# Twelve more hand-overs between the column steps of the block inverses and their transposes

## The chip, the core and the metric

The kernel runs on one core of a Trainium2 chip. Five engines work side by side, each through its own instructions in order: TensorE (PE in the profile, with its weight loads as PEld), VectorE (DVE), ScalarE (ACT), GpSimd (POOL) and SyncE (SP), which starts nearly all transfers. The metric is the device time of one execution in microseconds; lower is better.

## What is computed

One layer of a diffusion backbone on 1024 latent tokens and 256 context tokens, width 1024. An adaptive RMSNorm is followed by one projection of all 1280 tokens, whose columns feed two groups of heads: a gated DeltaNet (a convolution over five tokens, normalised q and k, and a scan over chunks of 64 tokens in the reference, forward and backward) and a neighbourhood attention on a grid 64 wide. An output projection and a SwiGLU feed-forward net follow. The piece around the change is the triangular system of each chunk:

```python
px = modulate(rms_norm(x, norm1_w[i]), sh1, sc1) @ w_in[i]
pc = modulate(rms_norm(ctx, norm1_w[i]), csh1, csc1) @ w_in[i]
...
m = jnp.where(strict, jnp.einsum("bhncd,bhnmd->bhncm", kb, k) * decay, 0.0)
a_mat = jnp.eye(CHUNK, dtype=f32) + m
u = lax.linalg.triangular_solve(a_mat, v * beta[..., None], left_side=True, lower=True, unit_diagonal=True)
w = lax.linalg.triangular_solve(a_mat, kb * jnp.exp(gam)[..., None], left_side=True, lower=True, unit_diagonal=True)
```

The kernel takes chunks of 128 tokens, so there are ten, two of context and eight of latents. It inverts the 32x32 blocks on the diagonal of each chunk's matrix first and builds the rest of the inverse from products of them.

## The kernel before, in words

**Projection.** The columns are worked through as a list of jobs (`jobs`). A Block is 128 columns of one kind: `k`, `q`, `v` and `z` belong to the DeltaNet, `nk` and `nq` to the attention. A Wide is a piece of the attention's values. Around the change they stand in this order: nk0, nk1, nk2, Wide, nk3, nq0, nq1, nq2, q0, q1, q2, q3. Each value is split in a high and a low part, and each product is made of three matmuls: high by high, low by high, high by low (`hh,whi`, `hl,whi`, `hh,wlo` in the rows). For nq and q a Block is eight steps over the 1024 rows (`KT`), with two column halves of 512 tokens, so 48 matmuls of 128x512 by the helper at L98 into two PSUM banks called `blk`, of which there are four.

**Around a Block.** At its start the weights of the job behind it are fetched: SP starts the load into `wraw` (L215; one buffer), ACT casts it to `whi` (L216; two buffers), and the low part `wlo` is made from it. At its end ACT empties the banks into `cacc` (L462). The normalisation of nk and nq squares `cacc` on ACT (L503), sums it in matmuls of `cr` with a constant `cst` into the PSUM banks called `m`, with one in a bank called `pr` for nk, takes Ln (L520) and Exp (L522, L524) of that on ACT, with table loads between them, multiplies on DVE (L527), casts on ACT (L532, L539), and SP stores it (L545). There are two banks `m`.

**Background work.** After each of the eight steps of a Block the loop calls `bg.step`, once up to q0 and three times from q1 on (`turn`); at each tile of a Wide it is called with 2, or 5. `bg` is a queue of generators; one step runs the first of them to its next `yield`, and what it issues up to there stands in program order at that place. The framework's scheduler then sets each engine's order from the program order and the dependences, without a time of its own for what a wait will cost.

The first generator is `block_inverses`. It transposes the 32x32 blocks into a layout in which 80 matrices times four blocks lie beside each other (`N`, on 80 partitions), and eliminates column by column on DVE: 30 steps of a multiply (L913) and an add (L915), with a `yield` after each. Then DVE sets the diagonal to one (L918), and there is one `yield`. Then come 32 transposes on PE (L102) out of that layout, four to a bank `m`, each bank emptied by an ACT copy into `WK` (L926), with a `yield` after each eight transposes. At last, for each of the two scan directions, DVE transposes (L932) and scales (L935), and SP stores both results in `x_d` in DRAM (L934, L937), with a `yield` after each direction.

The second generator is `preps`. It fetches decays `e` (L962), the products of keys `kk` (L963) and the block inverses `xc` (L964) of one chunk and direction; ACT copies `xc` into `fx` (L976) and takes the exponential of `e` (L980); DVE multiplies `kk` by it (L981); and PE makes the products `pr` (L98) that fill the inverse below its diagonal blocks, with an ACT copy (L991) and DVE copies between them. Only the four preps of the context chunks may begin before the blocks nq0 to q2 are done; the others wait for the last q block.

**Other transfers.** While nk3 and nq0 run, SP also issues the copies that gather the attention windows of the values (L1058, `vw_d` from `nv_d`).

Of the kernel before, what the change touches and what calls it, by code (L numbers as in the profile page):

```python
# [87 lines left out]
def hybrid(ctx, tc, a, dbg):  # L88
# [304 lines left out]
    with ExitStack() as bs:  # L393
# [459 lines left out]
        def block_inverses():  # L853
            with ExitStack() as gs:
# [61 lines left out]
                    yield  # L916
                flat = N.rearrange("p b r c -> p b (r c)")
                dve.memset(flat[:P, :, 0:1024:33], 1.0)  # L918
                yield
                U = WK.rearrange("p d u i -> p (d u) i")  # L920
                for i0 in range(0, 32, 4):
                    p = bank()
# [151 lines left out]
        for n in range(2, len(jobs) + 2):  # L1074
            j = jobs[n] if n < len(jobs) else None
            if n == inv:
                bg2.drain()
                bg2s.close()
                early.close()
                psum.append(bs.enter_context(tc.tile_pool(name="psa", bufs=1, space=PSUM)))  # L1080
                bg.add(block_inverses())
                bg.add(preps())
# [700 lines left out]
```

## Time and profile before

| what | value |
|---|---|
| three runs | 1526.71, 1526.71, 1532.21 us |
| median of the runs | 1526.71 us |
| the profiled execution, whole | 1526.16 us |
| its span in the trace | 1524.4 us |
| instructions in it | 23483 |
| PE busy, share of the span | 96% |
| DVE busy | 66% |
| ACT busy | 47% |
| POOL busy | 12% |
| mean granted clock of TensorE | 0.992 |

All times are microseconds from the span's start. A timeline row gives the start, the duration, the engine, the line, the operation, the output and the inputs by the program's names, the shape, how many equal instructions are grouped, and in brackets the engine's idle time ahead of it with what ended it. Matmuls overlap in the pipeline, so the pace of a series is read from the starts of its rows, not from the durations. A row of a window gives for each engine the busy share (the number of instructions that start in it), then the clock that the throttle granted to TensorE as a share of full speed, the share in which the DMA engines were busy, and GB/s. "blk L98" means output `blk`, line 98.

### The profile page before, as it was taken

The page shows a single profiled execution, that of the slowest core. Times are in us where ns is not written, and L with a number is a line of the kernel's source. Part 1 is how long each engine was busy: PE and PEld are TensorE (multiplying, and loading weights), DVE is VectorE, ACT ScalarE, POOL GpSimd, SP SyncE. Part 2 cuts the span into 40 slices and gives each one's busy share as a digit, 9 for nine tenths or more (in the row PEclk, how much of TensorE's full clock was granted, in tenths as well). Part 3 has the DMA queues.
Part 4 walks back from the last instruction along what each step waited for, and adds up shares of the span by engine and source line. Part 5 has one row for each costly group of instructions (what it writes and reads, how often), then busy time and mean ns, then how long its engine had stood idle before and what let it go on. Part 6 is the DMA issues. An engine that isn't in the chain of part 4 may idle for free.

```text
span 1524.4 us, 23483 instructions
## 1 busy us (share of the span) xinstructions
PE 1460.5 (96%) x8365; PEld 1206.5 (79%) x8365; DVE 1004.4 (66%) x1898; ACT 710.6 (47%) x1387; POOL 184.8 (12%) x253
## 2 busy tenths in 40 slices
PE   5999998999999999998899989999999999999998
PEld 3789787778877778887787878888888888888887
DVE  4787579354677427779986388765655556599642
ACT  5443362683366546566642374333333334354441
POOL 0154610342134300000100000000000000000000
PEclk9999999899999999999999999999999999999999
DMA  9377223654477789998539315333233335798742
GB/s 367 112 229 238 61 78 122 234 152 168 132 217 253 223 280 278 285 273 237 164 102 330 109 35 186 111 104 104 104 104 103 104 104 173 246 364 294 235 152 83
DMA packets 209830, 276.29 MB, mean 181 GB/s; under 512 B 15968, under 2 KB 116912, under 8 KB 208688
## 3 DMA queue, kind: packets, MB, share of 16 engines
q1 hardware_dynamic: 208992, 274.41, 55.7%
q8 instruction: 66, 1.08, 0.3%
q14 instruction: 52, 0.43, 0.1%
q10 hardware_dynamic: 720, 0.37, 0.1%
HBM read 209.93 MB, written 68.98 MB: 183 GB/s over the span
## 4 chain that ended last, share of the span: by engine, by line
PE 75%; DVE 11%; DMA 4%; issue 4%; ACT 4%; POOL 1%; SPq 0%; POOLq 0%; DVEq 0%; ACTq 0%
PE ps L98 50%; PE blk L98 12%; PE sc L98 4%; PE pr L98 3%; PE m L98 3%; PE sc L102 2%; DVE tt L913 2%; DVE N L915 2%; DVE cacc L471 1%; PE m L102 1%; PE pm L98 1%; ACT bt L340 1%; DVE bt L337 1%; DMA wad<-wa 1%; DMA wraw<-w_out 1%
## 5 line engine op out<-in xcount | busy, mean ns | idle before, releaser
L98 PE MATMUL ps<-hT,uhi 128*128 128x512 f32 x496 | 147.1, 391 | 3.1 <-ACT hT L1534 3.1
L98 PE MATMUL ps<-lT,uhi 128*128 128x512 f32 x496 | 146.3, 389 | 0.0
L98 PE MATMUL ps<-hT,ulo 128*128 128x512 f32 x496 | 146.2, 389 | 0.0
L98 PE MATMUL blk<-hh,whi 128*128 128x512 f32 (+1 forms) x456 | 139.5, 398 | 2.2 <-ACT hh L714 1.5
L98 PE MATMUL ps<-hB,uhi 128*128 128x512 f32 x436 | 129.7, 391 | 0.0
L98 PE MATMUL ps<-lB,uhi 128*128 128x512 f32 x436 | 129.3, 390 | 0.0
L98 PE MATMUL blk<-hh,wlo 128*128 128x512 f32 (+1 forms) x456 | 129.1, 377 | 0.0
L98 PE MATMUL ps<-hB,ulo 128*128 128x512 f32 x436 | 128.9, 389 | 0.0
L98 PE MATMUL blk<-hl,whi 128*128 128x512 f32 (+1 forms) x456 | 128.7, 376 | 0.0
L1410 ACT CAST uhi<-ws 128x512 fp32r<-128x512 f32 x91 | 54.8, 623 | 153.0 <-PE ps L98 87.6
L1410 ACT CAST uhi<-wq 128x512 fp32r<-128x512 f32 x101 | 60.6, 621 | 135.3 <-PE ps L98 73.4
L98 PEld LDWEIGHTS ps<-hT,uhi 128*128 128x128 f32 x496 | 93.1, 188 | 22.7 <-ACT hT L1534 3.5
L1411 DVE TENSOR_TENSOR ulo<-wq,uhi 128x512 fp32r<-128x512 f32 x101 | 67.4, 688 | 66.0 <-ACT uhi L1410 37.6
L98 PEld LDWEIGHTS ps<-lT,uhi 128*128 128x128 f32 x496 | 93.3, 188 | 19.5
L98 PEld LDWEIGHTS ps<-hT,ulo 128*128 128x128 f32 x496 | 93.1, 188 | 19.3
L98 PEld LDWEIGHTS ps<-hB,uhi 128*128 128x128 f32 x436 | 82.1, 188 | 17.6 <-issue 0.5
L98 PEld LDWEIGHTS ps<-lB,uhi 128*128 128x128 f32 x436 | 82.1, 188 | 17.1
L98 PEld LDWEIGHTS ps<-hB,ulo 128*128 128x128 f32 x436 | 81.8, 188 | 17.0
L98 PEld LDWEIGHTS blk<-hh,wlo 128*128 128x128 f32 x456 | 80.5, 190 | 17.7 <-issue 2.5
L98 PEld LDWEIGHTS blk<-hl,whi 128*128 128x128 f32 x456 | 81.0, 190 | 15.7
L98 PEld LDWEIGHTS blk<-hh,whi 128*128 128x128 f32 x456 | 77.6, 193 | 18.9 <-ACT hh L714 3.1
L337 DVE CUSTOM_DVE_ANT_0 bt<-sc,bt 128x640 f32<-128x640 f32 x64 | 52.5, 822 | 49.1 <-issue 39.4
(332 smaller groups left out, 3057.9 us busy)
## 6 DMA issues: line engine op xcount, KB each, us to landing
wq<-w_fo SPq DMA_DIRECT2D x99, 256.0 KB
wq<-w_gu SPq DMA_DIRECT2D x88, 256.0 KB
wad<-wa SPq DMA_DIRECT2D x64, 256.0 KB
bt<-rpb SPq DMA_DIRECT2D x64, 192.0 KB
t_d<-g SPq DMA_DIRECT2D x22, 512.0 KB
fr<-t_d SPq DMA_DIRECT2D x44, 256.0 KB
f_d<-g SPq DMA_DIRECT2D x33, 256.0 KB
fr<-f_d SPq DMA_DIRECT2D x33, 256.0 KB
```

The lines of the kernel that those rows point to most:

```text
L98: i = nc.tensor.matmul(*args, **kw)
L102: i = nc.tensor.transpose(*args, **kw)
L337: dve.tensor_tensor_reduce(bt, sc[:, u * 640:u * 640 + 640], bt, 1.0, -3.0e38, OP.add, OP.max, m[:, 0:1])
L340: act.activation(bt, bt, AF.Exp, bias=m[:, 1:2], accum_out=m[:, 2:3])
L471: dve.scalar_tensor_tensor(acc[:, d0:d1], p[:, d0 + o - s0:d1 + o - s0], cw[:, blk, tap:tap + 1], acc[:, d0:d1], op0=OP.mult, op1=OP.add)
L913: dve.tensor_tensor(t, N[:P, :, 0:c, c:c + 1].to_broadcast([P, 4, c, w]), N[:P, :, c:c + 1, c + 1:32].to_broadcast([P, 4, c, w]), OP.mult)
L915: dve.tensor_tensor(N[:P, :, 0:c, c + 1:32], N[:P, :, 0:c, c + 1:32], t, OP.add)
L1410: act.copy(hi, self.raw[key])
L1411: dve.tensor_tensor(lo, self.raw[key], hi.bitcast(F32), OP.subtract)
```

## The change

Where the generator of the block inverses gave back control once between the diagonal's memset and the transposes, it does so thirteen times.

```diff
                 flat = N.rearrange("p b r c -> p b (r c)")
                 dve.memset(flat[:P, :, 0:1024:33], 1.0)
-                yield
+                for _ in range(13):
+                    yield
                 U = WK.rearrange("p d u i -> p (d u) i")
                 for i0 in range(0, 32, 4):
                     p = bank()
```

No instruction is added or removed. With one background step per step of a Block, the transposes stand a block and a half later in the program, and all that follows in the queue, the stores of `x_d` and the preps, moves with them. Lines behind the change have a number that is one higher (the ACT copy L926 is L927).

The first place is PE at the transposes, in before. The `blk` rows are matmuls of the projection, `m<-cst,N` the transposes; these rows lie in the second half of block nq0.

```order
L98 MATMUL blk<-hh_139,wlo 128x512 x2
L98 MATMUL blk<-hh_414,whi 128x512
L102 MATMUL m<-cst,N 128x80 x2
L98 MATMUL blk<-hh_414,whi 128x512
L98 MATMUL blk<-hl_415,whi 128x512 x2
L102 MATMUL m<-cst,N 128x80 x6
L98 MATMUL blk<-hh_414,wlo 128x512
L102 MATMUL m<-cst,N 128x80 x8
L98 MATMUL blk<-hh_414,wlo 128x512
L102 MATMUL m<-cst,N 128x80 x8
L98 MATMUL blk<-hh_416,whi 128x512
L102 MATMUL m<-cst,N 128x80 x8
```

The same place in the program after the change, now in the last quarter of block nq1 (`hh_416` to `hh_420`); with the last two rows the next block, nq2, begins (`hh_133`), and `m<-cr,cst` is the sum of the normalisation of nq0. The last eight transposes stand four matmuls further on.

```order
L98 MATMUL blk<-hh_416,wlo 128x512 x2
L102 MATMUL m<-cst,N 128x80 x8
L98 MATMUL blk<-hh_418,whi 128x512 x2
L98 MATMUL blk<-hl_419,whi 128x512 x2
L98 MATMUL blk<-hh_418,wlo 128x512 x2
L102 MATMUL m<-cst,N 128x80 x8
L98 MATMUL blk<-hh_420,whi 128x512 x2
L98 MATMUL blk<-hl_421,whi 128x512 x2
L98 MATMUL blk<-hh_420,wlo 128x512 x2
L102 MATMUL m<-cst,N 128x80 x8
L98 MATMUL blk<-hh_133,whi 128x512 x2
L98 MATMUL m<-cr,cst 128x512 x2
```

From 25 matmuls of nq0 ahead of the first transpose it has become all 48 of nq0 and 36 of nq1, and the groups of eight stand six matmuls apart where they stood one apart.

The second place is ACT at the copies that empty the transposes' banks, in before; `cacc<-blk` empties a block, and the rows of L520 and L524 are the normalisation of nk3.

```order
L503 ACTIVATE cr<-cacc 128x1280
L926 COPY WK<-m 128x80x4 x8
L216 CAST whi<-wraw 128x1024
L462 ACTIVATE cacc<-blk 128x512 x2
L520 ACT_TABLE_LOAD
L520 ACTIVATE cr<-m,bias 128x256
```

The same stretch of ACT after the change.

```order
L503 ACTIVATE cr<-cacc 128x1280
L216 CAST whi<-wraw 128x1024
L462 ACTIVATE cacc<-blk 128x512 x2
L520 ACT_TABLE_LOAD
L520 ACTIVATE cr<-m,bias 128x256
L520 ACTIVATE cr<-m,bias 128x512
L520 ACTIVATE cr<-pr,bias 128x512
L503 ACTIVATE cr<-cacc 128x1024
L524 ACT_TABLE_LOAD
L524 ACTIVATE cr<-cr 128x1280
L532 CAST hl_2414<-cacc 128x1280
L927 COPY WK<-m 128x80x4 x4
```

The copies stood ahead of the cast of the weights of nq2 and now stand behind it and behind the whole normalisation of nk3.

The third place is PE at the first products of the preps. In before they stand at the start of block nq2 (`hh_133`), behind the sums of the normalisation of nq0.

```order
L98 MATMUL blk<-hh_420,wlo 128x512 x2
L98 MATMUL m<-cr,cst 128x512 x2
L98 MATMUL pr<-fx_2475,kk 128x96 x4
L98 MATMUL blk<-hh_133,whi 128x512 x2
L98 MATMUL blk<-hl_134,whi 128x512 x2
L98 MATMUL pr<-y_2471,kk 32x32 x4
```

After the change they stand behind the last matmul of block q0, within the sums of the normalisation of nq2.

```order
L98 MATMUL blk<-hh_420,wlo 128x512 x2
L98 MATMUL m<-cr,cst 128x512
L98 MATMUL pr<-fx_2608,kk 128x96 x4
L98 MATMUL m<-cr,cst 128x512
L98 MATMUL blk<-hh_133,whi 128x512
L98 MATMUL pr<-y_2604,kk 32x32 x4
```

They have moved past two whole blocks, nq2 and q0. From block q2 on PE's order is that of before again, since the later preps wait for the q blocks.

## The prediction

> **What bounds the kernel now.** The page comes first, for who is busy and whose work the end hangs on.
>
> ```profile
> PE 1460.5 (96%) x8365; PEld 1206.5 (79%) x8365; DVE 1004.4 (66%) x1898; ACT 710.6 (47%) x1387; POOL 184.8 (12%) x253
> PE 75%; DVE 11%; DMA 4%; issue 4%; ACT 4%; POOL 1%; SPq 0%; POOLq 0%; DVEq 0%; ACTq 0%
> ```
>
> TensorE is busy for 96% of 1524.4 us and carries 75% of the chain that ended last. The change adds no instruction, so it can move the time only through what PE waits for and the clock at which it works. PE's waits between 250 and 350 us come next.
>
> ```profile
> PE m L102 <- DVE N L918: 5.4, 1, 5.4
> PE pr L98 <- DVE kk L981: 1.9, 1, 1.9
> ```
>
> There are two: the first transpose of the block inverses waits for DVE's column steps, and the first product of the preps waits for the decayed keys. PE's timeline shows both, and the pace around them.
>
> ```profile
> 258.00 0.61 PE L98 MATMUL blk<-hh,whi 128*128 128x512 f32 x2
> 260.27 0.62 PE L98 MATMUL blk<-hh,wlo 128*128 128x512 f32 x2
> ...
> 266.52 0.53 PE L102 MATMUL m<-cst,N 80*128 80x80 f32 x2 [5.41 <-DVE N L918]
> ...
> 269.52 1.27 PE L102 MATMUL m<-cst,N 80*128 80x80 f32 x8
> 270.52 0.78 PE L98 MATMUL blk<-hh,wlo 128*128 128x512 f32 x1
> ...
> 275.64 0.63 PE L98 MATMUL blk<-hh,whi 128*128 128x512 f32 x2
> ...
> 278.41 1.45 PE L98 MATMUL m<-cr,cst 128*128 128x256 f32 x4
> ...
> 280.15 1.03 PE L98 MATMUL blk<-hh,whi 128*128 128x512 f32 x2
> ...
> 291.49 1.88 PE L98 MATMUL m<-cr,cst 128*128 128x512 f32 x4
> 295.27 1.62 PE L98 MATMUL pr<-fx,kk 128*128 128x96 f32 x8 [1.90 <-DVE kk L981]
> ```
>
> Ten matmuls go from 258.00 to 260.27, 0.227 us each. Behind the first wait eight transposes take 1.0 us (269.52 to 270.52). The windows of 1 us say why that is slow: the granted clock.
>
> ```profile
> 264.00:265.00 1.00, 0.00 (x0) 1.00 0.26 100
> 265.00:266.00 1.00, 0.00 (x0) 0.51 0.27 104
> 274.00:275.00 1.00, 1.00 (x3) 0.50 0.33 121
> 275.00:276.00 1.00, 1.00 (x5) 0.87 0.84 336
> 295.00:296.00 1.00, 0.73 (x5) 0.87 0.91 285
> 298.00:299.00 1.00, 1.00 (x10) 0.50 0.96 282
> 299.00:300.00 1.00, 1.00 (x12) 0.92 1.04 383
> ```
>
> The clock falls to half some 4 us into the first wait and stays there for about 8.7 us of work; it falls again right behind the 1.9 us wait and stays down for 3.5 us (to about 299.2). A wait costs PE its own length, and then half of every microsecond until the clock is back.
>
> **What goes.** Four terms, against the profiled execution of 1526.16 us (0.5 us under the median of 1526.71).
>
> The wait of 5.4 us: DVE is then done long before the transposes, since 12 steps more stand between.
>
> The slow work behind it: 266.52 to 275.64 is 9.1 us for 11 matmuls of 128x512 (11 x 0.227 = 2.5) and 32 transposes (at half their measured 1.0 per eight, 2.0). Loss: 4.6.
>
> The wait of 1.9, and half of the 3.5 us at half clock behind it: 1.75.
>
> Together 5.4 + 4.6 + 1.9 + 1.75 = 13.65 us less. This is all the change can win. 32 transposes, the products and the copies are still to be done.
>
> **What comes in its place.** The transposes now stand behind the other 23 matmuls of nq0, the sums of nk3's normalisation, and 36 matmuls of nq1. Without the wait PE goes on at 261.0: 23 x 0.227 = 5.2 to 266.2; the sums 1.7 (278.41 to 280.15) to 267.9; 36 x 0.227 = 8.2 to 276.1. But a transpose needs a bank `m`, of which there are two, both holding those sums until ACT has taken Ln of them. What ACT and SP do then is in their timelines and SP's waits.
>
> ```profile
> 257.01 1.27 ACT L503 ACTIVATE cr<-cacc 128x1280 f32<-128x1280 f32 x1
> ...
> 273.44 0.96 ACT L926 COPY WK<-m 128x320 f32<-128x320 f32 x2 [0.61 <-PE m L102]
> 278.83 1.04 ACT L216 CAST whi<-wraw 128x1024 fp32r<-128x1024 f32 x1 [4.43 <-DMA wraw<-w_nqk]
> ...
> 282.18 1.06 ACT L520 ACTIVATE cr<-m,bias 128x256 f32<-128x256 f32 x2
> ...
> 288.96 1.26 ACT L532 CAST hl<-cacc 128x1280 f16<-128x1280 f32 x1 [1.62 <-DVE cacc L527]
> ```
> ```profile
> 264.57 4.38 SPq L215 DMA_DIRECT2D wraw<-w_nqk  x1
> ...
> 274.43 0.33 SPq L934 DMA_DIRECT2D x_d<-WK  x1
> ```
> ```profile
> SPq L215 <- DMA wraw<-w_nqk: 0.9, 1, 0.9
> ```
>
> In before ACT stood 4.4 us at the cast of nq2's weights, which had landed only at 278.8, 14 us after their issue at 264.57. In that time the window copies hold a few DMA engines: 0.26 to 0.27 busy, 100 to 104 GB/s in the windows above. I take the same landing, because nothing ahead of that load on SP's queue moves. In before ACT had nothing else to do there. Now the copies out of `m` stand behind that cast, and so does the Ln that frees the banks. All that follows on ACT depends on work that PE has done by then, so it keeps the times of before.
>
> First wait: from 276.1 until the first Ln is over, 282.18 plus about 0.4 of the two Ln's 1.06: 282.6. That is **6.5 us**.
>
> Second wait: eight transposes fill both banks; the next eight need a copy to `WK`, which now stands behind the whole normalisation of nk3, whose last cast ends at 288.96 + 1.26 = 290.2. A copy takes 0.48 (two in 0.96), so 290.7. PE comes to this point at 282.6 + 1.0 for the transposes + six matmuls at half clock (six times 0.45 = 2.7) = 286.3. **4.4 us**.
>
> Half clock: all of 282.6 to 286.3, and from 290.7, if it lasts there as long as the total in before (8.7 us of work, less some that was spent), about 6.3 us more; half of 10.0 is **5.0 us**. Bounds: 3.5 us for a wait as short as 1.9 us and 8.7 for one of 5.4; with the first after the second wait half of 3.7 + 3.5 = 3.6, with the second half of 3.7 + 8.7 = 6.2. The second wait follows the first closely, so I stay between.
>
> Inside nq2 the last eight transposes wait for the two Ln's of the next normalisation: 0.3 each, **0.6 us**, from the 0.5 of an Ln. Bounds: nothing, and the 1.3 us of a table load on ACT that may stand ahead of them.
>
> The preps. From 290.7, 54 matmuls at 0.227 (12.3), the sums of nq0's normalisation (1.4, less than the 1.88 of their row, whose end overlaps), 24 transposes (1.5), 3.2 of half clock and the 0.6: nq2 ends at about 309.7. Sums of nq1's normalisation 1.4, block q0 10.9, one matmul 0.7: PE is at the first product at 322.7. When is it ready? The chain of waits shows what lies between.
>
> ```profile
> 277.50 4.29 DMA x_d<-ut
> ...
> 285.02 5.21 DMA x_d<-WK
> ...
> 290.25 3.75 DMA kk<-kk_d
> ...
> 295.27 1.62 PE pr L98 x8
> ```
>
> And DVE's first step behind the copies.
>
> ```profile
> 274.43 1.51 DVE L932 STREAM_TRANSPOSE ut<-WK 128x1280 f32<-128x1280 f32 x1 [7.10 <-ACT WK L926]
> ```
>
> In before 20.9 us pass from the last copy (274.4) to the first product (295.27): the transpose on DVE, the scaling, stores, fetches. The last copy in the new order stands in nq2, behind transposes that are done at about 303, thus at 304.0. Adding 20.9, 2.2 for being queued behind nq0's multiply and casts on DVE, and taking off up to 1 for a DMA queue less full, 325.9. PE waits about 3 us, with the rounding of the sums **2.8 us**. The bounds are nothing (the stores overlap better with nothing else queued) and 6 (each of three transfers some 1 us later). The clock behind it: 3.5 us at half after the 1.9 us wait; with a little less, **1.4 us**. Between the products stand only one or two matmuls now, and three products each wait 0.3 for ACT's or DVE's copies: **0.9 us**. Their work itself, like that of all the preps, is only moved into blocks behind, where PE has the same to do.
>
> Sum: 6.5 + 4.4 + 5.0 + 0.6 + 2.8 + 1.4 + 0.9 = 21.6 us come. 21.6 - 13.65 = 7.95, and 1526.16 + 7.95 = **1534.1 us**. Behind block q2 PE's order is that of before, and PE does not wait long enough there to take up a shift of 8 us, so what is lost stays lost.
>
> [...]
>
> **The rivals.** About 0.5% (7.6 us) is what a measurement of this kernel can tell from no change; that is 1519.1 and 1534.3 around the median.
>
> *The weights land earlier* (the other side). If the stores of `x_d`, which start at 274.43 in before, held up nq2's weights, these land sooner once the stores stand 30 us later, and the first two waits shrink microsecond by microsecond. At 272 the first two waits are some 6.7 us shorter in sum: 1527.4. At about 270.8 the change breaks even. For it: 14 us is long for one load of 512 KB. Against it: the stores were issued 10 us after the load, and the windows at 264 to 266 were at the same 100 to 104 GB/s without them. Time 1523.5 to 1529.5.
>
> *The waits go and nothing takes their place.* If ACT were ahead of the cast by then, only the waits on the preps and some clock would be left: 10 us less, 1516.2. Against it speaks ACT's order, which puts the copies behind that cast.
>
> *The preps come later still.* Should the stores and fetches of `x_d` now meet the loads of the q blocks' weights and the stores of nq, the products are ready 3 to 6 us later than I say, with the clock 5 to 11 us more: 1539.5 to 1545.
>
> *The clock is back sooner.* If the 3.5 us of half clock behind the 1.9 us wait, not the 8.7 behind the longer one, is what each of the two long waits costs, and the short wait ahead of the preps none, 1.5 of the 5.0 and the 1.4 go: 1531.2. For it: it happened so from 295.65 to 299.2, with PE full of work; against it: the longer wait is the nearer kin. [...]
>
> That the change does nothing is excluded: PE's order differs.
>
> **How the numbers follow.** My forecast 0.58, with a range of its own of 1529.5 to 1539.5 (clock 3.6 to 6.2, preps 0 to 6); the early weights 0.17; the clock back sooner 0.10; nothing in their place 0.05; later preps 0.10. The range 1524.0 to 1541.0 leaves out the case of nothing in their place, two thirds of the last and a little of the early weights. The forecast lies at the upper bound, so half of it counts as the same and half as slower: same 0.29 + 0.17 + 0.10 = 0.56, slower 0.29 + 0.10 = 0.39, faster 0.05.
>
> **What would show it.** PE's waits in the changed profile: the one for DVE at the transposes gone; one of about 6.5 us for ACT's Ln (L520) at the first transpose, one of 4.4 for the `WK` copy at the ninth, and one of about 2.8 before the first product. ACT should stand at the cast of nq2's weights until about 278.8; if it lands by 272, the first rival has it. The clock should be at half over 282 to 297 with little pause. Wrong would be a transpose that waits for nothing, or a loss that PE makes up before 350 us.

## The result, and the profile after

| | before | after |
|---|---|---|
| median of 12 runs | 1527.11 us | 1535.57 us |
| lowest and highest | 1523.68 and 1532.21 us | 1532.13 and 1538.67 us |
| span of the profiled execution | 1524.4 us | 1530.3 us |
| ratio, with its 95% interval | | 1.0046 (1.0035 to 1.0058) |

The ratio, taken from all runs of both, says that the change makes the kernel slower by 0.46%, which is 7 us, between 5.3 and 8.9. (The medians lie 8.5 us apart, the means 7.2.) The forecast was 1534.1 us.

PE's waits in the profile after, between 240 and 360 us (total, times, longest):

```profile
PE m L102 <- ACT cr L520: 6.2, 2, 5.9
PE m L102 <- ACT WK L927: 3.9, 1, 3.9
PE pr L98 <- DVE kk L982: 2.5, 1, 2.5
PE pr L98 <- DVE y L1000: 0.8, 1, 0.8
```

The wait for DVE at the transposes is gone. In its place the first transpose waits for ACT's Ln, the ninth for a copy into `WK`, both on ACT, and the first product of the preps still waits for its keys. PE's timeline puts them in their places:

```profile
279.86 1.38 PE L102 MATMUL m<-cst,N 80*128 80x80 f32 x8 [5.85 <-ACT cr L520]
...
282.82 1.05 PE L98 MATMUL blk<-hh,wlo 128*128 128x512 f32 x2
287.74 1.33 PE L102 MATMUL m<-cst,N 80*128 80x80 f32 x8 [3.87 <-ACT WK L927]
...
297.81 0.68 PE L102 MATMUL m<-cst,N 80*128 80x80 f32 x4 [0.34 <-ACT cr L520]
...
323.68 1.77 PE L98 MATMUL pr<-fx,kk 128*128 128x96 f32 x8 [2.52 <-DVE kk L982]
```

What ACT did in that time:

```profile
251.98 1.05 ACT L216 CAST whi<-wraw 128x1024 fp32r<-128x1024 f32 x1 [13.14 <-PE blk L98]
...
275.99 1.04 ACT L216 CAST whi<-wraw 128x1024 fp32r<-128x1024 f32 x1 [20.39 <-DMA wraw<-w_nqk]
...
279.33 1.05 ACT L520 ACTIVATE cr<-m,bias 128x256 f32<-128x256 f32 x2
...
286.10 1.26 ACT L532 CAST hl<-cacc 128x1280 f16<-128x1280 f32 x1 [1.62 <-DVE cacc L527]
287.26 0.75 ACT L927 COPY WK<-m 128x320 f32<-128x320 f32 x2
```

ACT stood 20.39 us at the cast of nq2's weights, where it stood 4.43 in before, and took the Ln and the copies only behind it. What SP had to issue:

```profile
250.04 11.60 SPq L1059 DMA_DIRECT2D vw_d<-nv_d  x6
261.74 4.38 SPq L215 DMA_DIRECT2D wraw<-w_nqk  x1
...
300.87 0.33 SPq L935 DMA_DIRECT2D x_d<-WK  x1
```

This execution ran 2.8 us ahead of the one of before when it came to this place (the load of nq2's weights at 261.74 against 264.57). With that taken off, the weights landed at the same moment as before (275.99 + 2.84 = 278.83), although the stores of `x_d` now come 26 us later (300.87 against 274.43). Of PE's clock three rows are enough:

```profile
276.00:277.00 1.00, 0.00 (x0) 0.59 0.00 0
...
292.00:293.00 1.00, 1.00 (x7) 0.50 0.00 0
293.00:294.00 1.00, 1.00 (x4) 0.87 0.00 0
```

It was at half from 276.2, some 2.2 us into the first wait, to 293.3, the second wait included.

A measure free of what differs elsewhere in an execution is the stretch on ACT from the cast of nq1's weights to that of v1's. In the profile before it ends here:

```profile
375.25 1.05 ACT L216 CAST whi<-wraw 128x1024 fp32r<-128x1024 f32 x1 [1.75 <-PE blk L98]
```

And after:

```profile
379.36 1.05 ACT L216 CAST whi<-wraw 128x1024 fp32r<-128x1024 f32 x1 [1.30 <-PE blk L98]
```

It is 375.25 - 254.67 = 120.6 us before and 379.36 - 251.98 = 127.4 after: 6.8 us more, which is nearly all of the 7. Below, "the stretch" is this.

### The profile page after: what moved, and what is told of

Its sections match the earlier page's. It is cut to its first block, busy times and chain, and to the rows that moved or that the text cites. A ratio compares the mean times of both kernels' runs of the same rounds, so it can differ in the third digit from the quotient of the medians.

```text
span 1530.3 us, 23481 instructions
## 1 busy us (share of the span) xinstructions
PE 1460.8 (95%) x8365; PEld 1205.9 (79%) x8365; DVE 1006.4 (66%) x1898; ACT 715.5 (47%) x1391; POOL 185.2 (12%) x253
## 4 chain that ended last, share of the span: by engine, by line
PE 71%; DVE 10%; DMA 6%; ACT 5%; issue 5%; POOL 1%; SPq 1%; ACTq 0%; POOLq 0%; DVEq 0%
PE ps L98 50%; PE blk L98 10%; PE sc L98 4%; PE pr L98 2%; PE m L98 2%; PE sc L102 2%; DVE cacc L471 1%; DMA wraw<-w_nqk 1%; DMA nv_d<-zt 1%; DVE tt L913 1%; DVE cacc L491 1%; DVE N L915 1%; DMA xt<-xcT 1%; DMA wad<-wa 1%; PE m L102 1%
```

## The experiments

The theory: the transposes cost nothing where they stand now; what costs is that ACT meets the cast of nq2's weights ahead of the work that frees the transposes' banks, and these weights land late behind the window copies. The rivals: the new place costs by itself (through the normalisation of nk3, which stands ahead of the copies too, or through the preps, which come later), or each hand-over costs a little.

**Spreading the window copies, first try.** In the kernel after (first run) and in before (second):

```diff
-                    copies.step(2)
+                    copies.step(1 if k % 4 == 0 else 0)
```

> The kernel after, with the sixteen window copies given out two per block instead of sixteen in one, so that the load of nq2's weights is no longer queued behind them. Theory (what the change costs is that the transposes' banks and copies stand behind a cast that waits for late weights): the two waits of 5.85 and 3.87 us at the transposes and the 4.7 us of half clock go, about 14.4 us less, 1521 us (1518 to 1524), with the wait of about 2.5 us before the first product still there. Rival (the place in the program itself costs, through ACT's normalisation or the later preps, and the weights only happen to land then): at most 3 us less, 1532 to 1536.

> The control: the kernel before with the same spreading of the window copies. Theory: PE waits for none of what comes earlier, since the 5.4 us wait is for DVE and the 1.9 us wait for the preps, so the same time, 1527 us, give or take 3. Rival (the burst of window copies slows the kernel whatever the change does): also some 10 us or more less, 1517 or below.

Measured: 1536.3 us, ratio to before 1.0042 (1.0027 to 1.0058), and 1527.76 us, ratio 0.9988 (0.9972 to 1.0003). Neither tells anything of the theory, because the edit did not reach the chip's order: the scheduler moved the copies forward again. SP in the first of the two:

```profile
252.55 11.60 SPq L1059 DMA_DIRECT2D vw_d<-nv_d  x6
264.24 4.38 SPq L215 DMA_DIRECT2D wraw<-w_nqk  x1
```

The six copies still stand right ahead of the load. What the two runs give is a second measurement of the change, and how far apart two kernels with the same work in the same order may come out: 0.12%.

**The copies held in their place.** The same edit, and the copies pinned to their place in program order, in after and in before:

```diff
-                    sp.dma_start(vw_d[:, cb, ch], vlat[4 * ch:4 * ch + 4, BLKS[cb]:BLKS[cb] + 32])
+                    tc.keep_in_program_order(
+                        sp.dma_start(vw_d[:, cb, ch], vlat[4 * ch:4 * ch + 4, BLKS[cb]:BLKS[cb] + 32]))
...
-                    copies.step(2)
+                    copies.step(1 if k % 4 == 0 else 0)
```

> The kernel after, with the window copies held to their place in program order and given out two per block, so that SP issues four of them ahead of the load of nq2's weights instead of sixteen; ACT's and PE's orders around the transposes stay those of the kernel after. Theory (the transposes wait because ACT stands at the cast of weights that land late): the cast comes right when nq0's last matmul frees its buffer, the first transpose waits for nothing, the ninth for less than 1 us, and the half clock goes with them: 5.85 + 3.87 + 4.7 = 14.4 us less than after, 1519 to 1524 us, which is also 0.2 to 0.5% less than before. Rival (the normalisation ahead of the copies holds them up by itself): the second wait of 3.9 us and its half clock stay, 1528 to 1532 us.

> The control: the kernel before with the window copies held and given out in the same way. Theory: PE waits there for DVE and for the preps, not for the weights, so 1527 us, give or take 3, with the wait of 5.4 us as it was. Rival (the burst of copies costs the kernel something else, which the early weights then win in both): 1515 to 1520 us.

Measured: 1528.47 us, ratio to before 1.0005 (0.9990 to 1.0021), and 1534.05 us, ratio 1.0033 (1.0019 to 1.0047). With early weights the order turns round: the kernel with thirteen hand-overs is 5.6 us faster than the one with one. PE's waits in the first:

```profile
PE blk L98 <- ACT cr L477: 3.9, 1, 3.9
...
PE m L98 <- DVE SQ L570: 1.8, 1, 1.8
...
PE m L102 <- ACT cr L520: 0.7, 2, 0.4
```

The 5.9 and the 3.9 us at the transposes are 0.7 in all: the theory holds, and the normalisation does not hold up the copies by itself. Yet the times lie 4.5 and 4 us above the expected ranges, and by its time alone the first would fit the rival; only its waits speak against that. In the first, new waits of 3.9 and 1.8 us come up some 100 us later. In the control, the copies now run beside the stores and fetches of the preps, and its wait before the first product is 5.85 us instead of 1.90 (with no copies there, in the next pair, it is 1.99). So the 5.6 us are what the control lost against before; the first, 0.4% faster than after, came out level with before. The control's wait:

```profile
297.71 2.02 PE L98 MATMUL pr<-fx,kk 128*128 128x96 f32 x8 [5.85 <-DVE kk L981]
```

**The copies held back altogether.** Pinned, given out two per step as before, but only from block z0 on, in after and in before; in a third kernel, after with twelve empty steps between the two generators:

```diff
-            if isinstance(j, Wide) and n == values:
+            if n == gates - 1:
...
                 bg.add(block_inverses())
+                bg.add(None for _ in range(12))
```

> The kernel after, with the window copies held back until block nq3 is done, so that no weights of a block between nk3 and nq3 stand behind them, and no store or fetch of the preps beside them. Theory (all that the change cost at the transposes was the late cast of nq2's weights): no wait over 0.5 us at the transposes, full clock there, the wait of about 2.5 us before the first product left; 14.4 us less than after, 1519 to 1524 us, and 6 to 8 us less than the kernel before with its copies held back alike. Rival (early weights only move the wait to a later block, as the spread copies did by about 6 us): 1527 to 1531 us.

> The control: the kernel before with the window copies held back in the same way. Theory: the wait of 5.4 us for DVE, the half clock behind it and the wait of about 1.9 us stay, 1527 us, give or take 3. Rival (the copies' place is worth something by itself, beyond the change): 1517 to 1522 us.

> As the kernel after with the window copies held back, and twelve empty steps between the block inverses and the preps. The first product then stands behind the first matmuls of q1 and the later ones further apart. Theory (the wait before the first product is the time of the stores and fetches of the block inverses, which a later place covers): the wait of about 2.5 us and the half clock behind it (1.7 us) shrink to about 1 us together, 2 to 4 us less than without the pause, 1516 to 1521 us. Rival (as in the kernel before with a pause, new waits come up between the products, where ACT is full): the same time as without the pause.

Measured: 1558.49, 1563.10 and 1557.70 us, ratios to before 1.0192 (1.0165 to 1.0218), 1.0224 (1.0197 to 1.0251) and 1.0184 (1.0156 to 1.0211). All three times miss, because the held copies now delay the weights of the last z blocks. ACT in the first of them:

```profile
547.15 1.05 ACT L216 CAST whi<-wraw 128x1024 fp32r<-128x1024 f32 x1 [12.62 <-DMA wraw<-w_z]
```

PE waits 18.5 us for casts there. This is far behind the stretch, which is now free of window copies, and so it is the cleanest comparison of all. In the kernel after:

```profile
253.64 1.05 ACT L216 CAST whi<-wraw 128x1024 fp32r<-128x1024 f32 x1 [13.14 <-PE blk L98]
264.92 1.05 ACT L216 CAST whi<-wraw 128x1024 fp32r<-128x1024 f32 x1 [7.67 <-PE blk L98]
...
369.26 1.05 ACT L216 CAST whi<-wraw 128x1024 fp32r<-128x1024 f32 x1 [1.37 <-PE blk L98]
```

And in the kernel before:

```profile
253.29 1.05 ACT L216 CAST whi<-wraw 128x1024 fp32r<-128x1024 f32 x1 [13.14 <-PE blk L98]
277.09 1.05 ACT L216 CAST whi<-wraw 128x1024 fp32r<-128x1024 f32 x1 [4.08 <-PE blk L98]
...
374.24 1.05 ACT L216 CAST whi<-wraw 128x1024 fp32r<-128x1024 f32 x1 [1.75 <-PE blk L98]
```

The cast of nq2's weights waits for PE to free its buffer, no longer for a load. The stretch of before is 374.24 - 253.29 = 121.0 us, as it was (120.6): the weights cost before nothing. That of after is 369.26 - 253.64 = 115.6 instead of 127.4: late weights cost it 11.8 us. The 14.4 that were expected did not come in full: from ACT's first copy of a product (L992) to the cast of q2's weights it took 11.98 us (314.24 to 326.22), where it took 10.70 in after (325.63 to 336.33), and that alone is 1.3 us. Without the late weights the change makes the stretch 5.3 us shorter, with them 6.8 us longer; the whole times of the two kernels without them lie 4.6 us apart, where 6 to 8 were expected. PE in the kernel after, from 272 to 282 us, is busy without a gap at full clock:

```profile
272.00:282.00 10.00, 10.00 (x57) 1.00 0.29 66
```

The pause of the third kernel brought nothing, as its rival had it: its stretch is 116.4 us, and its first product waits 2.65 us, now for an ACT copy.

**One copy per block.** The last run, meant to beat both kernels: after, with the copies pinned as above and one per block.

```diff
-                    copies.step(2)
+                    copies.step(1 if k == 0 else 0)
```

> A version that should beat both: the kernel after, with the window copies held to their place and given out one per block from nk3 on, so that no load has more than one copy right ahead of it and no burst of copies stands ahead of the last gates or the attention. Theory: the transposes wait for nothing, as with the copies held back, and the later weights land in time: 1519 to 1524 us, 0.3 to 0.6% less than before. Rival (any copy beside the stores and fetches of the preps delays these by as much as was won): 1527 to 1530 us.

Measured: 1525.86 us, ratio to before 0.9973 (0.9962 to 0.9983): faster than before by 0.27%, and than after by 0.7%. It lies 2 us above the expected range and 1 us below the rival's. Of its waits the two that answer to those of the spread copies:

```profile
PE blk L98 <- ACT cr L477: 1.9, 1, 1.9
...
PE m L102 <- ACT cr L520: 0.7, 2, 0.4
```

Between the two earlier ways: the later wait for `cr` is 1.9 us, where it was 3.9 with two copies per block, and no burst is left.

**Only the preps later.** Before, with its transposes where they were and twelve empty steps ahead of the preps:

```diff
                 bg.add(block_inverses())
+                bg.add(None for _ in range(12))
```

> The kernel before with the transposes where they were, and twelve empty steps between the block inverses and the preps, so that only the preps move. Theory: the wait of 1.9 us before the first product and the half clock behind it (1.75 us) go, and nothing comes: 3.6 us less than before, about 1523.5 us (1521 to 1526). Rival (later preps cost by themselves, by meeting the q blocks): 1529 us or more.

Measured: 1530.04 us, ratio 1.0006 (0.9990 to 1.0022). The expected gain did not come. The time as such lies in the rival's range, but before itself took 1528.83 us in these rounds, so the ratio shows no loss either. PE's waits:

```profile
PE m L102 <- DVE N L918: 5.4, 1, 5.4
PE pr L98 <- ACT kk L991: 3.1, 1, 3.1
PE pr L98 <- DVE kk L981: 1.2, 1, 1.2
```

The wait before the first product shrinks from 1.9 to 1.2 us, and one of 3.1 comes up between the products, for a copy on ACT. In the profiled execution the stretch is 2.6 us longer than in before (376.64 - 253.44 = 123.2), about as much as the waits have grown; the ratio allows for up to 3.4 us. Later preps by themselves do not win, and what they may lose is small.

**Fewer hand-overs.** Five in place of thirteen, and three:

```diff
-                for _ in range(13):
+                for _ in range(5):
```

> Five hand-overs instead of thirteen. The transposes then stand 12 matmuls later than before, but ACT's last copies come behind the cast of nq2's weights, and the sums of nk3's normalisation need the banks that these copies free. Theory: the wait for DVE is 2.5 instead of 5.4 us, but PE stands some 6 us at the sums of nk3, until the cast and a copy are over, with about 4 us of half clock behind each wait, and the last two copies come behind the whole normalisation, so that the preps are late by up to 10 us: 1538 to 1545. Rival (each step of delay takes its share of the wait for DVE, and a loss comes only once the transposes lie beyond nq0): 1522 to 1526.

> Three hand-overs alone, the control of the filled one: the first transpose is still behind 25 matmuls of nq0 and waits 5.4 us for DVE, all eight copies still stand ahead of the cast of nq2's weights, and the first product comes some 14 rows later, so that its wait of 1.9 us and the half clock behind it (1.75 us) go or turn into waits between the products. Theory: 1523 to 1528 us. Rival (the loss grows with each hand-over): 1528 to 1530 us.

Measured with five: 1535.88 us, ratio 1.0040 (1.0021 to 1.0058). PE's waits:

```profile
PE m L98 <- ACT WK L927: 5.4, 1, 5.4
PE m L102 <- DVE N L918: 2.9, 1, 2.9
PE pr L98 <- DVE kk L982: 2.6, 1, 2.6
PE pr L98 <- ACT kk L992: 1.9, 1, 1.9
```

The place of the wait is as expected: the sums of nk3 stand 5.4 us until a copy behind the cast frees a bank, and the rival, by which the loss comes only beyond nq0, falls. The time came out 2 us below the expected range; the preps wait 2.6 us and not up to 10.

Measured with three: 1535.08 us, ratio 1.0044 (1.0027 to 1.0061), where 1523 to 1528 was expected. All eight copies stand ahead of the cast here, the wait for DVE is the same 5.4 us, and yet the stretch is 381.36 - 254.38 = 127.0 us. Its waits:

```profile
PE m L102 <- DVE N L918: 5.4, 1, 5.4
PE pr L98 <- DVE kk L982: 3.9, 1, 3.9
PE pr L98 <- ACT kk L992: 2.5, 1, 2.5
```

What costs here is the preps: 3.9 us before the first product and 2.5 between them, 4.5 us more than before waits there, of the 6.4 by which the stretch is longer (127.0 less 120.6). Half clock behind both is the author's estimate for the rest; it was not shown. So the late cast is not the only way in which a few hand-overs can lose. The pause, with 1.2 and 3.1 us, lost far less, and DVE's order shows why. L932 and L933 are the transpose of the second scan direction, L527 the multiply of nk3's normalisation. With the pause:

```profile
280.83 1.51 DVE L932 STREAM_TRANSPOSE ut<-WK 128x1280 f32<-128x1280 f32 x1 [4.62 <-DMA x_d<-ut]
```

With three hand-overs:

```profile
286.78 1.55 DVE L527 SCALAR_TENSOR_TENSOR cacc<-cacc,qkw,cr 128x1280 f32<-128x1280 f32 x1 [7.23 <-ACT cr L524]
288.25 1.51 DVE L933 STREAM_TRANSPOSE ut<-WK 128x1280 f32<-128x1280 f32 x1
```

Here the transpose has come to stand behind that multiply, which waits for ACT's Exp. It comes 6.5 us later, counted from the start of the stretch, and with it the stores and fetches that the preps need. Three, five and thirteen hand-overs cost 0.44, 0.40 and 0.46%: the loss does not grow with their number, and the rival by which each costs a little falls.

**The wait filled with work.** Three hand-overs, and ahead of the transposes 24 matmuls whose result nobody reads:

```diff
+                p = bank("pr")
+                for _ in range(24):
+                    tc.keep_in_program_order(
+                        nc.tensor.matmul(p, mr[:, 2], hh[0][:, :512], start=True, stop=True))
                 U = WK.rearrange("p d u i -> p (d u) i")
```

> Three hand-overs instead of thirteen, so that the transposes stand where they stand in before, and 24 matmuls of 128x512 into a free bank that nobody reads, placed right ahead of the first transpose, where PE waits 5.4 us for DVE: work is added, none is left out. Theory (a wait costs its length and then half of every microsecond until the clock is back): the wait is still there as work, but the clock stays at full, so the 4.6 us of half clock behind it go: about 1522.5 us (1520 to 1525). Rival (the slow stretch is the transposes' own, by their shape or their weight loads): no gain, 1527 to 1530 us.

Measured: 1532.16 us, ratio 1.0024 (1.0014 to 1.0035). The control is the kernel with three hand-overs. PE in the filled one:

```profile
260.38 5.76 PE L924 MATMUL pr<-hh,mr 128*128 128x512 f32 x24
266.14 0.45 PE L102 MATMUL m<-cst,N 80*128 80x80 f32 x2
...
276.00 1.45 PE L98 MATMUL m<-cr,cst 128*128 128x256 f32 x4
...
303.98 2.02 PE L98 MATMUL pr<-fx,kk 128*128 128x96 f32 x8 [5.70 <-DVE kk L986]
```

And in the control:

```profile
266.19 0.53 PE L102 MATMUL m<-cst,N 80*128 80x80 f32 x2 [5.37 <-DVE N L918]
...
277.29 1.45 PE L98 MATMUL m<-cr,cst 128*128 128x256 f32 x4
```

The clock stayed at full through the transposes in the filled kernel (1.00 from 262 to 276 us; 0.50 in the control from 266 to 271), and PE did the work from the first transpose to the sums of nk3 in 9.86 us instead of 11.10: the slow stretch was the clock's, not the transposes'. But the 1.2 us won were given back at the first product, whose wait grew from 3.87 to 5.70 us: here too the transpose of the second direction stands behind the multiply of nk3's normalisation, and comes no earlier (288.58 us). The stretch is 127.0 us in both. The time of 1532.16 us misses both expectations, which were reckoned from before; against the control the medians lie 2.9 us apart, with intervals that overlap; what that difference is, if it is one, the traces don't show.

## Why the prediction was right

*What goes.* The 5.4 us wait and its half clock are gone: PE is busy without a gap until 274.0 us of the profile after. As forecast.

*The first wait*, forecast 6.5 us: 5.85. The cast landed at the moment of before, the assumption on which this stood. That the window copies set that moment was argued only from 0.26 and 100 GB/s in the prediction; the runs with the copies out of the way showed it.

*The second wait*, forecast 4.4: 3.87, behind the normalisation's cast at 286.10, as forecast.

*Half clock at the transposes*, forecast 5.0: at work 4.0 us (279.86 to 283.87) and 5.5 us (287.74 to 293.26), half of which is 4.8. The two bounds given, 3.5 and 8.7 us, were right to be kept apart, but that the clock came back between them is in part luck: its lengths in before and after were all multiples of 3.41 us (last section), which the prediction did not know.

*The waits in nq2*, forecast 0.6: 0.34.

*The preps*, forecast 2.8, 1.4 and 0.9 (for the 2.8 the working itself, 325.9 less 322.7, gives 3.2): the wait is 2.52; the half clock behind it lasts 3.4 us, so 1.7; one later wait has 0.78.

Sum: 5.85 + 3.87 + 4.8 + 0.34 + 2.52 + 1.7 + 0.78 = 19.9, less 13.65, is 6.2 us; the stretch gives 6.8, the ratio 7.0, and 7.95 was forecast. Each term but one that comes was a little too large. Of what goes, the half clock at the transposes in before was 4.4 rather than 4.6 us (half of the 8.75 us of work until 275.27).

*The rivals.* That the stores of `x_d` had held up the weights is refuted: stored 26 us later, they left the landing where it was. The point from which that rival would decide (weights early enough, and the change wins) was right, and the runs reached it by another way: 5.3 us less in the stretch once the window copies were gone. Preps later by 3 to 6 us did not come. The clock was back sooner than after the long wait of before (8.75 us of work), but not as soon as in 3.5 us behind the second wait (5.5), and behind the short wait ahead of the products (2.52 us) it was at half again for 3.4 us.

*What the prediction did not say* is that the place of the transposes was a good one, and the order of the weights on SP the thing to mend. It priced the change as given and looked no further.

## What to carry to other kernels

Work that is moved to fill a wait takes its place in the queues of all engines that it uses: look on each of them for the next instruction ahead of it that waits for a transfer; here ACT stood 20.39 us at the cast of nq2's weights, and PE 5.85 and 3.87 us for what ACT took up behind it. Before a wait is called the price of a move, ask why the thing waited for is late: here a burst of copies that only the attention reads, some 270 us later, stood ahead of 512 KB that were needed at once. And a wait that is cut on a chain with another wait behind it can be given back there: that happened with the filled wait (3.87 us became 5.70) and with the pause (1.9 became 1.2, and 3.1 came up).

## What the runs showed of the hardware that was not expected

The length of half clock behind a wait wasn't a constant, nor did it grow with the wait alone. Behind 5.4 us of waiting it took PE about 8.7 us of work to get the full clock back in before, where single matmuls stand between the groups of eight transposes, and about 5.8 us with three hand-overs, where six matmuls stand between most of them; behind 3.87 us of waiting in after it took 5.5. Useless matmuls in the wait kept the clock at full (1.00 from 262 to 276 us).

Windows of 0.1 us on the traces of before and after show a step. In before the clock is at half from 265.03 to 275.27 us (10.24 us), from 295.75 to 299.16 (3.41), and for 3.41 us three times elsewhere; in after from 276.19 to 293.26 (17.07), from 323.99 to 327.40 (3.41), and for 3.41 and 6.83 us elsewhere (the last microseconds of each execution aside). All these lengths are multiples of 3.41 us, and so are the distances between the changes within each of the two: from 275.27 to 295.75 in before it is 20.48 us, six times 3.41, and from 293.26 to 323.99 in after 30.73, nine times. The windows with three hand-overs give 6.8 us at half (265.16 to 271.98). The 8.7 us of work in before are the rest of the 10.24, whose first 1.5 us PE still waited. Behind the wait before the first product it was 3.41 us both in before (1.90 us of waiting) and in after (2.52 us). That where a wait falls on the step counts as well as its length is the author's guess; no run was made that shows it.

A window copy took SP 1.93 us to issue in the burst (11.60 us for six) and 0.65 us alone; what the rest of that time went to, no row names.

```profile
250.79 0.64 SPq L1060 DMA_DIRECT2D vw_d<-nv_d  x1
258.07 0.60 SPq L215 DMA_DIRECT2D wraw<-w_nqk  x1
```

These rows are from the kernel after with two held copies per block, where the load of nq2's weights takes 0.60 us to issue instead of 4.38.
